# Where the output layers' seven products are added up: through copies and GpSimd, or straight from the accumulators on VectorE

## The chip, the cores and the metric

The kernel runs on one core of one Trainium2 chip. A core has five engines that work side by side, each through a queue of its own in order: TensorE (PE; matrix products, whose weight loads the profile lists as PEld), VectorE (DVE), ScalarE (ACT), GpSimd (POOL) and SyncE (SP), which here issues nearly all DMAs. Products land in PSUM, in eight banks of 128 x 512 float32; the other data live in SBUF. The metric is the device time of one execution in microseconds; lower is better.

## The reference, cut to what matters

One layer of a hybrid decoder runs over 1024 prompt columns and 8 sample columns (1032 in all, held as features x columns). Two of its four steps are SwiGLU networks with a residual:

```python
def swiglu(x, wi, wo):
    g, u = jnp.split(x @ wi, 2, axis=-1)
    return (jax.nn.silu(g) * u) @ wo

x = layer_norm(ALPHA * x + 0.5 * swiglu(x, ffn1_wi, ffn1_wo), ln_g[0], ln_b[0])
...
x = layer_norm(ALPHA * x + 0.5 * swiglu(x, ffn2_wi, ffn2_wo), ln_g[2], ln_b[2])
```

D_MODEL is 1024, the hidden width 2816. The change is in the output layer, the product with `wo`, and in how its result reaches the scaled residual `ALPHA * x`.

## The kernel before

**Precision.** Every float32 operand is split into a rounded part and a remainder ("hi" and "lo"), and each product is three matmuls: hi·hi, hi·lo, lo·hi (lines 432 to 434 in `product`, 172 to 174 in `unit`). Splitting costs a ScalarE cast (L258, L148, L588) and a VectorE subtraction (L259, L149, L589).

**Seven products in place of eight.** Most layers treat a 2 x 2 arrangement of blocks by a Strassen-Winograd scheme: two halves of the output features (i = 0, 1) and two column blocks (s and s + 2) from seven products instead of eight. There are four column blocks (`BLK4`, of 256, 260, 256 and 260 columns), so one "pair" treats s = 0 and s = 1: seven products, each for two s. `wcomb` makes the seven weight tiles of a pair from four raw blocks: seven splits, two VectorE sums (L267, L270) and two GpSimd ones (L268, L275).

**A pair before (`pair`).** Products 0, 2 and 5 accumulate in one bank A, products 4 and 6 in one bank E, products 1 and 3 have banks of their own (`aux`). Partial sums of A and E are needed too, so ScalarE copies them out to SBUF ("snapshots", L450, L457, L461, L465). The four outputs of an s are each a VectorE sum of a snapshot and a bank:

- output 0, block s: snapshot of P0, plus P1 (L454)
- output 1, block s: A = P0 + P2 + P5, less the snapshot of P3 (L469)
- output 1, block s + 2: A plus the snapshot of P4 (L470)
- output 0, block s + 2: E = P4 + P6, plus the snapshot of P0 + P2 (L474)

Banks: tag `mm` has four, `aux` three, `pn` one. `pair` takes its long accumulators A and E with `mm`, four per pair, so A of the next pair takes the bank of this pair's A. `unit_ps` hands out `mm` four times of five and `pn` the fifth time.

**The output layer (`ffn`, `segment`).** The hidden rows come back from HBM in groups of two or three pairs of 128-row tiles (`groups`), already in the seven combined forms, and are split (`split_load`, L588 and L589). Each group adds to all 1024 output features in four segments of 256 (n = 0 to 3); each segment loads its raw weights (L603), combines them and runs one pair, whose products are three or two tiles deep, so nine or six matmuls for each product and s. The residual stands in eight tiles `RT`, loaded (L595) and scaled by ALPHA on ScalarE (L596). The `out` of a segment lets VectorE write the output into a temporary tile and GpSimd add that to the residual (L610). There are three groups in each of two networks, hence 24 such pairs with eight outputs each. The rest of the hidden rows is added by plain products after that, in `ounit`, where VectorE adds the bank to the residual directly (L632).

A scheduler that simulates the engines' time line orders the instructions of each queue; `tc.high_priority()` puts what stands in it ahead of other work that is ready. Waits between engines are added from the data each touches; a whole bank counts as one.

Of the kernel before, what the change touches and what calls it, by code (L numbers as in the profile page):

```python
# [12 lines left out]
OP = mybir.AluOpType  # L13
# [17 lines left out]
BN = (256, 260)  # L31
BM = 260
BLK4 = [(i // 2 * HW + i % 2 * BN[0], BN[i % 2]) for i in range(4)]
# [3 lines left out]
def F_(ap):  # L37
    return ap.bitcast(F32)
# [25 lines left out]
def layer_kernel(ctx: ExitStack, tc: tile.TileContext, I, O):  # L64
    nc = tc.nc
    V, S, G, T, DQ = nc.vector, nc.scalar, nc.gpsimd, nc.tensor, nc.sync
# [10 lines left out]
    def gen(i, dt=F32, n=NT):  # L77

        tag = f"a{i}" if isinstance(i, int) else i
        return sb.tile([128, 1024 if tag in WN else 4 * BM], dt, name=tag, tag=tag)[:, :1024 if tag in WN else n]  # L80
# [14 lines left out]
    def tmp(n=BM):  # L95
        return tmpp.tile([128, BM], F32, name="tmp", tag="tmp")[:, :n]
# [3 lines left out]
    def mm(n=512):  # L100
        return psp.tile([128, 512], F32, name="mm", tag="mm", bufs=NMM)[:, :n]

    def unit_ps(n=512):

        turn["n"] += 1
        return mm(n) if turn["n"] % 5 else psp.tile([128, 512], F32, name="pn", tag="pn", bufs=1)[:, :n]
# [3 lines left out]
    def aux(n=512):  # L110
        return psp.tile([128, 512], F32, name="aux", tag="aux", bufs=7 - NMM)[:, :n]
# [20 lines left out]
    def slot():  # L132
        s = ring["slots"][ring["i"] % len(ring["slots"])]
        ring["i"] += 1
        return gen(s, R)
# [27 lines left out]
    def wrow(w, rows, half, dst=None):  # L163

        t = [wload(w[r:r + 128, half * 512:(half + 1) * 512].rearrange("p (k n) -> p k n", n=128), 4, 128,
                   gen(dst[i], R) if dst else None) for i, r in enumerate(rows)]
        return [[(hi[:, j, :], lo[:, j, :]) for hi, lo in t] for j in range(4)]
# [15 lines left out]
    def bs(t, b, blk=BLK):  # L183
        c0, n = blk[b]
        return t[:, c0:c0 + n]
# [17 lines left out]
    def xparts(X7, j, kp):  # L203
        t = X7[j][kp // 2]
        return t[:, 2 * (kp % 2)], t[:, 2 * (kp % 2) + 1]
# [43 lines left out]
    def wcomb(raws):  # L249

        lo_, up = raws
        g = lo_.shape[1]
        a11, a21, a12, a22 = lo_[:, :, 0:128], lo_[:, :, 128:256], up[:, :, 0:128], up[:, :, 128:256]

        def put(src):
            s = slot()
            hi, lo = (s[:, i * 512:i * 512 + g * 128].rearrange("p (k n) -> p k n", n=128) for i in range(2))
            S.copy(hi, src)  # L258
            V.tensor_tensor(lo, src, F_(hi), op=OP.subtract)  # L259
            return hi, lo  # L260

        def fresh():
            return rawp.tile([128, 512], F32, name="raw", tag="raw")[:, :g * 128].rearrange("p (k n) -> p k n", n=128)

        s1, s2, s3 = fresh(), fresh(), fresh()
        out = [put(a11)]
        V.tensor_tensor(s1, a21, a22, op=OP.add)  # L267
        G.tensor_tensor(s3, a11, a21, op=OP.subtract)  # L268
        out.append(put(a12))
        V.tensor_tensor(s2, s1, a11, op=OP.subtract)  # L270
        out.append(put(s2))
        out.append(put(a22))
        out.append(put(s1))
        s4 = fresh()
        G.tensor_tensor(s4, a12, s2, op=OP.subtract)  # L275
        out.append(put(s3))
        out.append(put(s4))
        return out
# [150 lines left out]
    def product(ps, w, xs, start, stop):  # L429
        for kp, (xh, xl) in enumerate(xs):  # L430
            wh, wl = (t[:, kp] for t in w)
            T.matmul(ps, wh, xh, start=start and kp == 0, stop=False, skip_group_check=True)  # L432
            T.matmul(ps, wh, xl, start=False, stop=False, skip_group_check=True)  # L433
            T.matmul(ps, wl, xh, start=False, stop=stop and kp == len(xs) - 1, skip_group_check=True)  # L434
# [3 lines left out]
    def pair(ws, XS, subs, out, first=False):  # L438

        live = {}  # L440

        def step(j, s):
            w = ws[j]
            xs = XS(j, s) if callable(XS) else [xparts(XS[s], j, kp) for kp in range(4)]
            P = live.setdefault(s, {})
            snap = [SN["v"][i][s] for i in range(4)]
            if j == 0:
                P["A"] = mm(BN[s])
                product(P["A"], w, xs, True, False)
                order_["snap"] = S.copy(snap[0], P["A"]).ins  # L450
            elif j == 1:
                ps = aux(BN[s])
                product(ps, w, xs, True, True)
                out(0, s, lambda d: V.tensor_tensor(d, snap[0], ps, op=OP.add))  # L454
            elif j == 2:
                product(P["A"], w, xs, False, False)
                order_["snap"] = S.copy(snap[1], P["A"]).ins  # L457
            elif j == 3:
                ps = aux(BN[s])
                product(ps, w, xs, True, True)  # L460
                order_["snap"] = S.copy(snap[2], ps).ins  # L461
            elif j == 4:
                P["E"] = mm(BN[s])
                product(P["E"], w, xs, True, False)
                order_["snap"] = S.copy(snap[3], P["E"]).ins  # L465
            elif j == 5:
                A = P["A"]
                product(A, w, xs, False, True)
                out(1, s, lambda d: V.scalar_tensor_tensor(d, snap[2], -1.0, A, op0=OP.mult, op1=OP.add))  # L469
                out(1, s + 2, lambda d: V.tensor_tensor(d, snap[3], A, op=OP.add))  # L470
            else:
                E = P["E"]
                product(E, w, xs, False, True)
                out(0, s + 2, lambda d: V.tensor_tensor(d, snap[1], E, op=OP.add))  # L474


        for j, s in [(j, s) for js in ((0, 1), (2, 3, 4, 5, 6)) for s in subs for j in js] if first else \
                [(j, s) for j in range(7) for s in subs]:
            step(j, s)
            with tc.issue_after(order_["snap"]):  # L480
                for f in beside.pop(0) if beside else ():
                    f()

    def ffn(wi, wo, l, XS, enter, xlate, raws, sgs, RTs, res, groups, plains, tail, extra=None):
# [37 lines left out]
        def wi_raw(p, k):  # L522
            i = 2 * p + k
            return wraw(wi, k * FF + p * 256, raws[2 * (i % 2):2 * (i % 2) + 2])
# [51 lines left out]
        for p in range(1, NHID // 2):  # L576
            for k in range(2):
                w = w0 if p == 1 and k == 0 else wcomb(wi_raw(p, k))
# [13 lines left out]
        RT = []  # L592
# [5 lines left out]
        def segment(ps_, parts, n, i):  # L598
            g = len(ps_)
            rw = []  # L600
            for q in range(2):
                t = gen(raws[2 * (i % 2) + q])[:, :g * 256].rearrange("p (k n) -> p k n", n=256)
                DQ.dma_start(t, wo[ps_[0] * 256:(ps_[0] + g) * 256, n * 256:(n + 1) * 256].rearrange(  # L603
                    "(k t p) n -> t p k n", t=2, p=128)[q])
                rw.append(t)

            def out(i, c, fn):
                t, r = tmp(BN[c % 2]), bs(RT[2 * n + i], c, BLK4)
                fn(t)
                G.tensor_tensor(r, r, t, op=OP.add)  # L610

            pair(wcomb(rw), lambda j, s: [tuple(bs(u, s, BLK4) for u in parts[j, k]) for k in range(g)], (0, 1), out)

        i = 0
        for ps_, slots in groups:
            parts = {}
            for j in range(7):
                for k, p in enumerate(ps_):
                    t = gen(slots[j * len(ps_) + k], R)
# [14 lines left out]
        for gi, rows_ in enumerate(plains):  # L634
# [10 lines left out]
            else:  # L645
                if extra:
                    r = ring["slots"][ring["i"] % 9:] + ring["slots"][:ring["i"] % 9]
# [102 lines left out]
    ps = aux()  # L750
# [3 lines left out]
    ps = aux()  # L754
# [170 lines left out]
    def lin_store(dst, d, n, sm):  # L925
        for i in range(2):
# [5 lines left out]
            if sm is not None:  # L932
# [6 lines left out]
    parts = {0: [(0, 26, 27), (1, 0, 1)], 2: [(7, 31, 32), (6, 10, 11)],  # L939
             1: [(0, 2, 3), (1, 8, 9)], 3: [(7, None, None), (6, 28, 29)]}  # L940
# [13 lines left out]
    for c in (0, 2, 1, 3):  # L954
        for k in range(2):
            for i in range(2):
                if len(wp) < 4:
                    wp.append(wcol(w_in, (Q0, K0)[k] + i * 128))
                ps = unit_ps(BLK4[c][1])
# [310 lines left out]
    for i in (34, 29, 20, 21):  # L1270
        t = gen(i, R, 4 * BM).rearrange("p (i t e) -> p i t e", i=2, e=BM)[:, :, :, 0:258]
# [126 lines left out]
    def wa_in(t, m):  # L1398
        s = gen((18, 28, 23)[m % 3]).rearrange("p (d n) -> p d n", n=516)
        DQ.dma_start(s[:, 0], ascr[m][:, half_cols(t)])  # L1400
        DQ.dma_start(s[:, 1], tbscr[m][:, half_cols(t)])
        return s, wcol(I["w_a"][0], m * 128)
# [34 lines left out]
    ps = aux()  # L1437
# [25 lines left out]
    for m in range(0, 8, 2):  # L1463
        u = [wa_in(1, m + i) for i in range(2)]
# [10 lines left out]
    for m in range(8):  # L1475
        for b in range(3):
            ps = unit_ps(BLK[b][1])
            unit(ps, wa[m // 4][m % 4], cols(MH[:K2], ML[:K2], b))
            r = bs(r2[m], b)
            V.scalar_tensor_tensor(r, r, ALPHA, ps, op0=OP.mult, op1=OP.add)  # L1480
    rows = [k * 128 for k in range(K2, 8)]
    w = wrow(w_mix, rows, 0, r_[0:5] + [18])
# [280 lines left out]
    t = gen(21, R)  # L1763
# [51 lines left out]
```

## Time and profile before

| | |
|---|---|
| time of three runs | 2703.46, 2705.56, 2705.60 us; median 2705.56 |
| profiled execution | 2706.57 us, of which the span of the profile is 2704.8 |
| granted TensorE clock | 0.996 of full speed |
| the 24 GpSimd-added pairs | L610 runs from 467.9 to 638.2 us and from 2324.5 to 2506.7 us, 96 times in each |

The span runs from the first to the last instruction of the profile; the rest of the execution lies around it. A row of grouped instructions gives line, engine, operation, output and inputs, shape and count, then busy time in us and the mean of one in ns, then the engine's idle time just before them with what ended it.

### The profile page before, as it was taken

The numbers are of one execution on the slowest core, as the hardware profiler recorded it, in microseconds if no ns is written. First come the engines' busy times: TensorE is split into PE (matmuls) and PEld (weight loads), VectorE is DVE, ScalarE is ACT, GpSimd is POOL, SyncE is SP. The second block draws the span as 40 slices with busy tenths as digits, with TensorE's granted clock in tenths as the row PEclk, the third lists the DMA queues.
The fourth block names the chain that finished last, engine by engine and source line by source line (L and its number), as shares of the span: only waits on it lengthen the run. The fifth ranks groups of instructions, "written<-read, shape, count | busy, mean of one in ns | idle before, by whom it ended". The sixth has DMA issues, their size and how long they took to land.

```text
span 2704.8 us, 56720 instructions
## 1 busy us (share of the span) xinstructions
PE 2647.3 (98%) x21775; PEld 2610.3 (97%) x21775; DVE 1856.5 (69%) x3932; ACT 1341.6 (50%) x3031; POOL 830.1 (31%) x840
## 2 busy tenths in 40 slices
PE   9999999999999999999999999999999999999998
PEld 9999999999999999999999999999999999999888
DVE  6755556887885756646666677758855555788887
ACT  5544446554554445446666555425544444655351
POOL 2222221565421111111111334323322222465554
PEclk9999999999999999999999999999999999999999
DMA  6333236432332434236657776731433323643211
GB/s 206 103 108 107 89 104 209 145 120 69 102 107 88 122 98 126 79 88 181 183 176 230 244 231 220 249 100 32 161 100 106 102 90 109 214 150 119 81 46 58
DMA packets 311928, 355.18 MB, mean 131 GB/s; under 512 B 28536, under 2 KB 246344, under 8 KB 311656
## 3 DMA queue, kind: packets, MB, share of 16 engines
q1 hardware_dynamic: 289336, 330.30, 38.4%
q10 hardware_dynamic: 22320, 21.26, 2.7%
q8 instruction: 170, 2.79, 0.4%
q14 instruction: 102, 0.84, 0.1%
HBM read 246.09 MB, written 105.42 MB: 130 GB/s over the span
## 4 chain that ended last, share of the span: by engine, by line
PE 37%; DVE 6%; DMA 4%; issue 2%; ACT 2%; POOL 1%; SPq 0%; DVEq 0%; ACTq 0%; POOLq 0%
PE mm L432 5%; PE mm L433 5%; PE mm L434 5%; PE mm L172 4%; PE mm L174 4%; PE mm L173 4%; PE aux L433 2%; PE aux L434 2%; PE aux L432 2%; PE pn L174 1%; PE pn L172 1%; DMA a<-in_w_in_dram 1%; PE pn L173 1%; DVE a L212 1%; DMA a<-yscr 1%
## 5 line engine op out<-in xcount | busy, mean ns | idle before, releaser
L432 PE MATMUL mm<-a,w 128*128 128x256 f32 (+1 forms) x2402 | 680.5, 284 | 9.4 <-DVE tmp L470 5.9
L433 PE MATMUL mm<-a,w 128*128 128x256 f32 (+1 forms) x2402 | 676.8, 282 | 1.2 <-DVE a L212 1.2
L434 PE MATMUL mm<-a,w 128*128 128x256 f32 (+1 forms) x2402 | 675.2, 281 | 0.0
L432 PEld LDWEIGHTS mm<-a,w 128*128 128x128 f32 x2402 | 452.6, 188 | 15.9 <-DVE tmp L470 7.6
L433 PEld LDWEIGHTS mm<-a,w 128*128 128x128 f32 x2402 | 453.0, 189 | 2.1 <-DVE a L212 1.6
L434 PEld LDWEIGHTS mm<-a,w 128*128 128x128 f32 x2402 | 452.6, 188 | 0.1
L275 POOL TENSOR_TENSOR raw<-a,raw 128x512 f32<-128x512 f32 (+2 forms) x98 | 125.4, 1279 | 949.5 <-issue 443.9
L259 DVE TENSOR_TENSOR w<-raw,w 128x512 fp32r<-128x512 f32 (+2 forms) x258 | 185.6, 721 | 203.5 <-ACT w L258 201.1
L432 PE MATMUL aux<-a,w 128*128 128x260 f32 (+1 forms) x1000 | 283.1, 283 | 3.9 <-DVE a L454 3.0
L433 PE MATMUL aux<-a,w 128*128 128x260 f32 (+1 forms) x1000 | 282.1, 282 | 0.0
L434 PE MATMUL aux<-a,w 128*128 128x260 f32 (+1 forms) x1000 | 282.1, 282 | 0.0
L432 PE MATMUL mm<-a,e 128*128 128x256 f32 (+1 forms) x812 | 230.1, 283 | 1.6 <-DVE tmp L474 1.1
L433 PE MATMUL mm<-a,e 128*128 128x256 f32 (+1 forms) x812 | 229.0, 282 | 0.8 <-DVE a L212 0.8
L434 PE MATMUL mm<-a,e 128*128 128x256 f32 (+1 forms) x812 | 228.6, 281 | 0.0
L610 POOL TENSOR_TENSOR a<-a,tmp 128x256 f32<-128x256 f32 (+1 forms) x192 | 178.9, 959 | 86.8 <-DVE tmp L454 37.8
L174 PE MATMUL mm<-a,w 128*128 128x256 f32 (+4 forms) x715 | 201.5, 285 | 0.0
L172 PE MATMUL mm<-a,w 128*128 128x256 f32 (+3 forms) x671 | 191.7, 287 | 4.0 <-ACT w L148 1.7
L432 PEld LDWEIGHTS aux<-a,w 128*128 128x128 f32 x1000 | 188.9, 189 | 5.4 <-DVE a L454 4.0
L258 ACT CAST w<-a 128x512 fp32r<-128x512 f32 (+2 forms) x200 | 117.5, 587 | 149.7 <-PE mm L434 93.6
L173 PE MATMUL mm<-a,w 128*128 128x256 f32 (+3 forms) x671 | 190.6, 285 | 0.0
L434 PEld LDWEIGHTS aux<-a,w 128*128 128x128 f32 x1000 | 189.1, 189 | 0.0
L433 PEld LDWEIGHTS aux<-a,w 128*128 128x128 f32 x1000 | 189.1, 189 | 0.0
(508 smaller groups left out, 7790.9 us busy)
## 6 DMA issues: line engine op xcount, KB each, us to landing
a<-in_ffn_wi_dram SPq DMA_DIRECT2D x80, 512.0 KB
a<-in_w_in_dram SPq DMA_DIRECT2D x68, 512.0 KB
a<-hsum SPq DMA_DIRECT2D x119, 258.0 KB
hsum<-a SPq DMA_DIRECT2D x68, 258.0 KB
a<-in_ffn_wo_dram SPq DMA_DIRECT2D x40, 384.0 KB
a<-in_state_C_dram ACTq DMA_DIRECT2D x32, 256.0 KB
out_dram<-a ACTq DMA_DIRECT2D x32, 256.0 KB
raw<-in_w_b_dram SPq DMA_DIRECT2D x32, 256.0 KB
```

The source lines that it names most:

```text
L172: T.matmul(ps, wh, xh, start=(i == 0), stop=False)
L173: T.matmul(ps, wh, xl, start=False, stop=False)
L174: last = T.matmul(ps, wl, xh, start=False, stop=(i == n - 1))
L212: order_["lo"] = V.tensor_tensor(dst[1], src, F_(dst[0]), op=OP.subtract).ins
L258: S.copy(hi, src)
L259: V.tensor_tensor(lo, src, F_(hi), op=OP.subtract)
L275: G.tensor_tensor(s4, a12, s2, op=OP.subtract)
L432: T.matmul(ps, wh, xh, start=start and kp == 0, stop=False, skip_group_check=True)
L433: T.matmul(ps, wh, xl, start=False, stop=False, skip_group_check=True)
L434: T.matmul(ps, wl, xh, start=False, stop=stop and kp == len(xs) - 1, skip_group_check=True)
L610: G.tensor_tensor(r, r, t, op=OP.add)
```

## The change

`segment` no longer uses `pair`. It runs the same 14 products in the same order and adds every accumulator, or partial accumulator, straight into the residual on VectorE, at high priority: product 0 into output 0 of block s, product 1 too; A after product 2 into output 0 of block s + 2; product 3 subtracted from output 1 of block s; product 4 into output 1 of block s + 2; A after product 5 into both blocks of output 1; E after product 6 into output 0 of block s + 2. The snapshots, temporaries and GpSimd additions of these pairs are gone. A and E come from `unit_ps`, so from five banks in turn. The pairs of other layers keep `pair`.

```diff
-            def out(i, c, fn):
-                t, r = tmp(BN[c % 2]), bs(RT[2 * n + i], c, BLK4)
-                fn(t)
-                G.tensor_tensor(r, r, t, op=OP.add)
-
-            pair(wcomb(rw), lambda j, s: [tuple(bs(u, s, BLK4) for u in parts[j, k]) for k in range(g)], (0, 1), out)
+            w = wcomb(rw)
+
+            def add(i, c, ps, op=OP.add):
+                r = bs(RT[2 * n + i], c, BLK4)
+                with tc.high_priority():
+                    V.tensor_tensor(r, r, ps, op=op)
+
+            A, E = {}, {}
+            for j, s in [(j, s) for j in range(7) for s in range(2)]:
+                if j in (0, 4):
+                    (E if j else A)[s] = unit_ps(BN[s])
+                ps = (aux(BN[s]) if j % 2 and j < 5 else E[s] if j in (4, 6) else A[s])
+                product(ps, w[j], [tuple(bs(u, s, BLK4) for u in parts[j, k]) for k in range(g)],
+                        j not in (2, 5, 6), j not in (0, 2, 4))
+                if j == 3:
+                    add(1, s, ps, OP.subtract)
+                elif j == 5:
+                    add(1, s, ps)
+                    add(1, s + 2, ps)
+                else:
+                    add(int(j == 4), s + 2 if j in (2, 4, 6) else s, ps)
```

## The prediction

> **What bounds the kernel now.** I read the page's busy time first, then the table by stretch around the two output layers, then what TensorE waited for in them.
>
> ```profile
> PE 2647.3 (98%) x21775; PEld 2610.3 (97%) x21775; DVE 1856.5 (69%) x3932; ACT 1341.6 (50%) x3031; POOL 830.1 (31%) x840
> ```
>
> TensorE (PE) is busy for 98% of the span, so the change can only pay where TensorE stands still. The changed code runs in two places: 12 pairs of column blocks from about 455 to 640 us (first output layer), 12 from about 2319 to 2507 us (second). The table by stretch (length, then busy time and instruction count of PE, PEld, VectorE, ScalarE, GpSimd) cuts the first where its pairs shrink from three tiles deep to two.
>
> ```profile
> 480.00:590.00 110.00, 106.98 (x893) 106.17 (x892) 94.20 (x158) 61.02 (x142) 69.29 (x72) 1.00 0.44 144
> 590.00:634.00 44.00, 40.25 (x320) 38.45 (x318) 38.35 (x66) 23.47 (x61) 28.13 (x34) 1.00 0.21 71
> 480.00:634.00 154.00, 147.23 (x1211) 144.63 (x1209) 132.55 (x223) 84.50 (x202) 97.43 (x105) 1.00 0.38 123
> 2345.00:2500.00 155.00, 150.21 (x1252) 149.02 (x1251) 124.08 (x207) 81.29 (x191) 93.62 (x97) 1.00 0.38 123
> ```
>
> The granted clock is 1.00 throughout, so the clock costs nothing here. VectorE (DVE) works 132.55 of 154 us in the first layer (86%) and 124.08 of 155 in the second (80%): it is the second-busiest engine, and its queue runs in order. What TensorE waited for, first layer and then second (total, times, longest):
>
> ```profile
> PE mm L432 <- DVE tmp L470: 3.6, 6, 1.2
> PE mm L432 <- DVE tmp L474: 1.8, 2, 1.1
> PE aux L432 <- DVE tmp L454: 0.9, 1, 0.9
> PE mm L432 <- ACT sreg L457: 0.5, 1, 0.5
> ...
> PE mm L432 <- DVE tmp L470: 4.5, 4, 1.3
> PE mm L432 <- ACT sreg L465: 0.3, 1, 0.3
> ```
>
> The chief row is L470, the last read of accumulator A: 10 stalls, 8.1 us, because the next pair's A wants that bank. One of them, from the timelines of PE, VectorE and GpSimd (start, duration):
>
> ```profile
> 524.52 0.28 PE L434 MATMUL aux<-a,w 128*128 128x260 f32 x1
> 525.83 0.39 PE L432 MATMUL mm<-a,w 128*128 128x260 f32 x1 [1.03 <-DVE tmp L470]
> ...
> 522.97 1.12 DVE L589 TENSOR_TENSOR a<-a 128x516 fp32r<-128x516 f32 x1
> 524.01 1.09 DVE L259 TENSOR_TENSOR w<-raw,w 128x384 fp32r<-128x384 f32 x1
> 525.02 0.41 DVE L469 SCALAR_TENSOR_TENSOR tmp<-sreg,mm 128x260 f32<-128x260 f32 x1
> 525.36 0.41 DVE L470 TENSOR_TENSOR tmp<-sreg,mm 128x260 f32<-128x260 f32 x1
> ...
> 522.80 1.89 POOL L610 TENSOR_TENSOR a<-a,tmp 128x256 f32<-128x256 f32 x2 [0.96 <-DVE tmp L469]
> ```
>
> The reads sat behind two subtractions of 1.12 and 1.09 us that ran beside two GpSimd additions. Matmul durations overlap, so stalls are better counted from starts:
>
> ```profile
> 495.41 0.28 PE L432 MATMUL aux<-a,w 128*128 128x260 f32 x1
> ...
> 496.48 0.28 PE L432 MATMUL mm<-a,w 128*128 128x256 f32 x1
> ```
>
> Nine matmuls of 260 columns take 1.07 us start to start, with 256 columns 256/260 of that: 0.118 us each on average. At that pace 893, 320 and 1252 matmuls need 105.4, 37.8 and 147.7 us; of the three stretches TensorE therefore loses **4.6, 6.2 and 7.3 us, 18.1 in all**. Idle time alone says 3.0 + 3.8 + 4.8 = 11.6 (a stall of 1.03 us shows 1.31 − 0.12 = 1.19 between starts). Between 11.6 and 18.1 lies the most that the change can remove there.
>
> **The change part by part.** A pair is seven products for each of two column blocks. *Removed per pair:* eight copies of partial sums on ScalarE, eight GpSimd additions, and the second VectorE operand from the copies. *Added:* VectorE goes from eight instructions that read an accumulator to sixteen. Products, weights and DMAs stay; nothing moves past SP's or GpSimd's queue.
>
> ScalarE and GpSimd first.
>
> ```profile
> L450 ACT COPY sreg<-mm 128x260 f32<-128x260 f32 (+1 forms) x21 | 7.8, 373 | 10.1 <-PE mm L434 9.2 <-DVE tmp L469 0.8
> ...
> L610 POOL TENSOR_TENSOR a<-a,tmp 128x260 f32<-128x260 f32 (+1 forms) x86 | 78.7, 942 | 30.6 <-DVE tmp L469 15.3 <-DVE tmp L454 9.1 <-DVE tmp L474 6.1
> ```
>
> In 154 us of the first layer ScalarE loses about 86 copies × 0.373 = 32 us and GpSimd 78.7 of its 97.43 us (81%). Neither sets the end (84.50 and 97.43 busy of 154), so by themselves both count nothing; what is late next is VectorE.
>
> VectorE pays. The same form, accumulator added into a resident tile, already runs at L632:
>
> ```profile
> L632 DVE TENSOR_TENSOR a<-a,mm x71: 401/420/542, 638.7 to 2561.7; 128x256 f32<-128x256 f32 x26, 128x260 f32<-128x260 f32 x26, 128x384 f32<-128x384 f32 x13, 128x264 f32<-128x264 f32 x6
> ```
>
> It lasts 0.42 us, but back to back such instructions start 0.34 us apart (525.02 and 525.36 above). There are as many new ones as there were GpSimd additions: 86 × 0.34 = **29.2 us more** for VectorE in the first layer's stretch, 80 × 0.34 = 27.2 in the second's.
>
> It gets part of that back, since its subtractions run longer beside GpSimd. Their rows between 480 and 634 us, and the shortest of each kind:
>
> ```profile
> L589 DVE TENSOR_TENSOR a<-a 128x516 fp32r<-128x516 f32 x36 | 30.5, 864 | 2.5 <-ACT a L588 2.1
> L259 DVE TENSOR_TENSOR w<-raw,w 128x384 fp32r<-128x384 f32 (+1 forms) x27 | 18.6, 693 | 6.5 <-ACT w L258 5.5 <-PE mm L434 1.1
> L259 DVE TENSOR_TENSOR w<-a,w 128x384 fp32r<-128x384 f32 (+1 forms) x21 | 18.0, 857 | 0.1
> L270 DVE TENSOR_TENSOR raw<-raw,a 128x384 f32<-128x384 f32 (+1 forms) x10 | 8.0, 797 | 0.0
> L267 DVE TENSOR_TENSOR raw<-a,a 128x384 f32<-128x384 f32 (+1 forms) x9 | 7.2, 799 | 3.3 <-POOL raw L275 3.2
> ...
> L589 DVE TENSOR_TENSOR a<-a x119: 677/692/1515, 430.0 to 2454.5; 128x516 fp32r<-128x516 f32 x119
> L259 DVE TENSOR_TENSOR cd<-raw,cd 128x384 fp32r<-128x384 f32 x4 | 2.2, 550 | 1.6 <-ACT cd L258 1.6
> ```
>
> Against 0.677 and 0.550 us undisturbed: 36 × 0.187 + 27 × 0.143 + 21 × 0.307 + 10 × 0.247 + 9 × 0.249 = 6.7 + 3.9 + 6.4 + 2.5 + 2.2 = 21.7 us. That is a lower bound, because some of the last 67 are only 256 wide; were all of them, an undisturbed one would last 0.55 × 256/384 = 0.37 us (an estimate) and the sum be 33.8. L610 is 81% of GpSimd's time, so **17.6 to 27.4 us come back**. I take 24, nearer the upper end since whole pairs are 256 wide in the second stretch. VectorE then needs 132.55 + 29.2 − 24 = 138 us, against 142.9 us of matmuls (1211 × 0.118): 97%. The ends are 134.4 and 144.2, and 161.8 if the lengthening has another cause. In the second layer, with the same return for each addition, it needs 124.08 + 27.2 − 22 = 129 of 147.7 (87%).
>
> [...]
>
> Waits. *Bank release:* long accumulators now rotate through five banks, four of them taken per pair, so the next pair's first A finds a bank free since the pair before last, and its second waits for a read four products back instead of three. That is the L470 stall, and it goes. *New waits:* product 2 adds into A, so it must wait for the addition after product 0, and product 6 likewise for that after product 4. ScalarE did these reads before (0.5 and 0.3 us of stalls); now they stand in VectorE's queue. That makes four waits per pair, with three products of cover: 3.2 us at depth three, 2.1 at depth two. Behind a late one TensorE holds everything. I price a stall at 0.81 us (8.1 / 10) plus the 0.26 that idle time hides (1.19 + 0.10 for the slow restart, against 1.03): 1.07 us. Unseen in this trace, their number is bounded by 0 and all 96; the additions are put at high priority and the subtractions ahead of them get shorter, so I take three, 3.2 us. *The residual tile* must be there for the first addition: it is.
>
> ```profile
> 453.58 1.07 ACT L596 ACTIVATE a<-a 128x1032 f32<-128x1032 f32 x1 [0.16 <-DMA a<-xscr]
> ...
> 464.89 0.63 ACT L450 COPY sreg<-mm 128x256 f32<-128x256 f32 x2
> ```
>
> Scaled by 454.7 us in the first layer, the first tile is ready ten microseconds before the first product's sum is read.
>
> **The sum.** Stalls removed where VectorE has room: 4.6 + 7.3 = 11.9. From 590 to 634 us, depth two, VectorE is at 38.35 of 44 and has the same work left over for less TensorE time: I count nothing of the 6.2. Less 3.2 for new stalls: −8.7. The span of 2704.8 becomes 2696.1; the profiled execution took 2706.57, 1.8 more than its span and 1.0 more than the median of 2705.56. So 2696.1 + 1.8 − 1.0 = **2696.9 us**.
>
> **The rivals.** *Slower: VectorE's additions become the tight wait.* L470 stalled 10 of its 48 times under a cover of three products. If the 80 new waits at depth three do so at that rate (17) and half the 16 at depth two (8), that is 25 × 1.07 = 26.8 us against 18.1 removed: 2705.6 + 8.7 = 2714 us. It decides above 17 stalls of 96. For it: VectorE at 97%. Against: shorter subtractions, priority.
>
> *No change: VectorE is simply full in the first layer*, its 144.2 us at the low return taking whatever TensorE saves, and only the second gains, 7.3 − 3.2: 2701.5 us. [...]
>
> *More: nothing is late any more.* All 18.1 us go: 2687.5 us. It needs the full return of shared time.
>
> **How the numbers follow.** Forecast 0.45, full VectorE 0.24, slower 0.18, all gone 0.13. A measurement of this kernel can tell about 0.2% (5.4 us) from no change: faster 0.45 + 0.13 = 0.58, same 0.24, slower 0.18. The range runs from just under the all-gone case to just short of the slow one, 2686 to 2713.
>
> **What would show it.** Right: no stall on the last reader of A; L589 near 0.70 and L259 at 384 near 0.55 us; GpSimd's time in 480 to 634 down to about 19 us; VectorE at 134 to 144 us there. Wrong: waits of mm on the new addition in more than 17 places, subtractions still at 0.85 us, or waits of TensorE on L259 or L149, the weights that VectorE would then bring late.

## The result, and the profile after

The changed kernel takes 2692.17 us (median of five executions, 2685.85 to 2695.54) against 2705.56 for the kernel before (2703.46 to 2707.96): a ratio of 0.9948, with a 95% interval of 0.9932 to 0.9964. That is 13.4 us off; 8.7 were forecast. A second set of the same kernel (e5 below) gave 2691.71 and 0.995 [0.9938, 0.9961]. The profiled execution took 2685.85 us, with a span of 2684.0: it was the fastest of the five, 6.3 below the median, so its time is not compared with the 2706.57 of before.

First the page's busy time:

```profile
PE 2638.3 (98%) x21775; PEld 2604.1 (97%) x21775; DVE 1871.4 (70%) x4124; ACT 1287.8 (48%) x2839; POOL 652.8 (24%) x648
```

TensorE has the same 21775 matmuls. VectorE gained 192 instructions (eight for each of 24 pairs) but only 15 us of busy time; ScalarE and GpSimd each lost 192 instructions. Next the table by stretch in the first output layer, with the columns as before (length; busy time and count of PE, PEld, VectorE, ScalarE, GpSimd; granted clock):

```profile
480.00:590.00 110.00, 107.79 (x898) 106.65 (x897) 97.89 (x216) 47.20 (x89) 14.12 (x14) 1.00 0.45 148
590.00:634.00 44.00, 43.54 (x356) 42.45 (x357) 41.36 (x106) 13.97 (x29) 5.46 (x8) 1.00 0.28 87
480.00:634.00 154.00, 151.33 (x1253) 149.10 (x1253) 139.25 (x321) 61.18 (x118) 19.58 (x22) 1.00 0.40 130
```

At 0.118 us per matmul, TensorE now loses 110 − 898 × 0.118 = 4.0 us in the first stretch (4.6 before) and 44 − 356 × 0.118 = 2.0 in the second (6.2 before). Nearly all of this layer's gain lies behind the point where the pairs shrink to two tiles. VectorE is at 139.25 of 154 us, 90%. Its groups there:

```profile
L612 DVE TENSOR_TENSOR a<-a,mm 128x256 f32<-128x256 f32 (+1 forms) x108 | 42.3, 412 | 7.0 <-PE mm L434 6.8
L589 DVE TENSOR_TENSOR a<-a 128x516 fp32r<-128x516 f32 x34 | 24.8, 741 | 2.2 <-ACT a L588 2.2
L612 DVE TENSOR_TENSOR a<-a,aux 128x260 f32<-128x260 f32 (+1 forms) x43 | 17.2, 412 | 1.4 <-PE aux L434 1.3
...
L259 DVE TENSOR_TENSOR w<-a,w 128x384 fp32r<-128x384 f32 (+1 forms) x21 | 10.2, 490 | 0.4 <-ACT w L258 0.2
L612 DVE TENSOR_TENSOR a<-a,pn 128x260 f32<-128x260 f32 (+1 forms) x25 | 10.1, 412 | 0.9 <-PE pn L434 0.9
```

L612 is the new addition, 176 times in this stretch. The subtractions of L589 went from a mean of 0.864 to 0.741 us, those of the weights (`w<-a,w`) from 0.857 to 0.490. Much of the idle time ahead of L612 is now spent waiting for TensorE, which is what one wants to see. What TensorE waited for, first layer:

```profile
PE mm L432 <- DVE a L612: 2.0, 4, 0.8
PE pn L432 <- DVE a L612: 0.3, 1, 0.3
PE aux L432 <- DVE a L612: 0.2, 1, 0.2
```

And from 2290 to 2500 us, the second (L172 is a matmul of the plain products behind the pairs):

```profile
PE mm L432 <- DVE a L612: 2.4, 5, 0.8
...
PE mm L172 <- DVE a L612: 0.8, 1, 0.8
...
PE pn L432 <- DVE a L612: 0.3, 1, 0.3
```

So 13 stalls wait for the new addition, 6.0 us of idle time in all, 0.46 each. (In the second list five more, 1.8 us, wait for additions of the plain products, and aren't shown.) Before, the rows shown ahead of the result have 13 stalls on VectorE's reads as well (ten on L470, two on L474, one on L454), 10.8 us, 0.83 each: the stalls became shorter, not fewer. One of them, from the timelines of TensorE and VectorE (start, duration):

```profile
529.38 0.28 PE L434 MATMUL mm<-a,w 128*128 128x260 f32 x1
530.43 0.36 PE L432 MATMUL mm<-a,w 128*128 128x256 f32 x1 [0.77 <-DVE a L612]
...
528.19 0.68 DVE L589 TENSOR_TENSOR a<-a 128x516 fp32r<-128x516 f32 x1
528.80 0.54 DVE L259 TENSOR_TENSOR w<-a,w 128x384 fp32r<-128x384 f32 x1
529.27 0.68 DVE L589 TENSOR_TENSOR a<-a 128x516 fp32r<-128x516 f32 x1
529.87 0.41 DVE L612 TENSOR_TENSOR a<-a,mm 128x260 f32<-128x260 f32 x1
```

It is the same picture as the stall shown of before, with shorter subtractions: no instruction here is stretched (0.68 and 0.54 us are the undisturbed lengths), yet three of them stand ahead of the addition.

The columns tell what kind of stall it is. A new wait, such as that of product 2 for the addition after product 0, lies within one accumulator, so the addition and the product have equally many columns, 256 for s = 0 and 260 for s = 1. A bank that is handed on goes to the other s here: four of the five banks are taken per pair, so a bank moves on by one place in the order A, A, E, E (s = 0, 1, 0, 1) from pair to pair, and the three `aux` banks alternate likewise. Above, a product of 256 columns waits for an addition of 260: it waits for a bank. In the timelines that holds for 10 of the 13 stalls, some 5.1 of the 6.0 us. Only three (at 592.95, 2366.59 and 2428.80 us; 0.9 us together) have equal columns and so are new waits. The stall on `pn`, of which there is one bank, can be followed whole:

```profile
517.84 0.28 PE L434 MATMUL pn<-a,w 128*128 128x260 f32 x1
527.01 0.35 PE L432 MATMUL pn<-a,w 128*128 128x256 f32 x1 [0.31 <-DVE a L612]
...
526.45 0.41 DVE L612 TENSOR_TENSOR a<-a,pn 128x260 f32<-128x260 f32 x1
```

The first row is the last matmul of product 5 into an A, the last row the fourth and last addition that reads this A, 8.3 us after that matmul ended. TensorE did eight other products (72 matmuls) in between and still came to a bank that wasn't free. The remaining long stalls lie at 527 to 530, 587 to 593, 2366 to 2372 and 2429 to 2434 us, where VectorE splits the next group's hidden rows (L589).

### The profile page after: what moved, and what is told of

It is laid out like the page before. It is cut to its first block, busy times and chain, and to the rows that moved or that the text cites. A ratio compares the mean times of both kernels' runs of the same rounds, so it can differ in the third digit from the quotient of the medians.

```text
span 2684.0 us, 56381 instructions
## 1 busy us (share of the span) xinstructions
PE 2638.3 (98%) x21775; PEld 2604.1 (97%) x21775; DVE 1871.4 (70%) x4124; ACT 1287.8 (48%) x2839; POOL 652.8 (24%) x648
## 4 chain that ended last, share of the span: by engine, by line
PE 79%; DVE 9%; DMA 5%; ACT 2%; issue 2%; POOL 1%; SPq 0%; ACTq 0%; DVEq 0%; POOLq 0%
PE mm L432 13%; PE mm L433 13%; PE mm L434 13%; PE aux L432 5%; PE aux L434 5%; PE aux L433 5%; PE mm L172 5%; PE mm L174 5%; PE mm L173 5%; PE pn L172 1%; PE pn L173 1%; PE pn L174 1%; DVE a L212 1%; DVE a L589 1%; DVE w L259 1%
## 5 line engine op out<-in xcount | busy, mean ns | idle before, releaser
L432 PE MATMUL mm<-a,w 128*128 128x260 f32 (+1 forms) x2313 | 654.9, 283 | 3.4 <-DVE a L612 2.5
L433 PE MATMUL mm<-a,w 128*128 128x260 f32 (+1 forms) x2313 | 651.0, 282 | 0.9 <-DVE a L212 0.9
L434 PE MATMUL mm<-a,w 128*128 128x260 f32 (+1 forms) x2313 | 649.9, 281 | 0.0
L432 PEld LDWEIGHTS mm<-a,w 128*128 128x128 f32 x2313 | 435.3, 188 | 9.0 <-issue 3.7
L433 PEld LDWEIGHTS mm<-a,w 128*128 128x128 f32 x2313 | 435.7, 188 | 1.5 <-DVE a L212 1.3
L434 PEld LDWEIGHTS mm<-a,w 128*128 128x128 f32 x2313 | 435.3, 188 | 0.1
L259 DVE TENSOR_TENSOR w<-raw,w 128x512 fp32r<-128x512 f32 (+2 forms) x258 | 174.6, 678 | 189.5 <-ACT w L258 188.2
L432 PE MATMUL mm<-a,e 128*128 128x260 f32 (+1 forms) x785 | 222.5, 283 | 0.9 <-DVE a L612 0.6
L433 PE MATMUL mm<-a,e 128*128 128x260 f32 (+1 forms) x785 | 221.2, 282 | 0.7 <-DVE a L212 0.7
L434 PE MATMUL mm<-a,e 128*128 128x260 f32 (+1 forms) x785 | 220.8, 281 | 0.0
L174 PE MATMUL mm<-a,w 128*128 128x256 f32 (+3 forms) x739 | 208.0, 284 | 0.2 <-DVE w L149 0.2
L172 PE MATMUL mm<-a,w 128*128 128x260 f32 (+4 forms) x695 | 198.0, 286 | 3.2 <-DVE a L647 1.7
L173 PE MATMUL mm<-a,w 128*128 128x260 f32 (+4 forms) x695 | 197.0, 285 | 0.0
L258 ACT CAST w<-raw 128x512 fp32r<-128x512 f32 (+2 forms) x258 | 152.2, 591 | 65.6 <-PE aux L434 21.6
```

The lines of the kernel that those rows point to most:

```text
L172: T.matmul(ps, wh, xh, start=(i == 0), stop=False)
L173: T.matmul(ps, wh, xl, start=False, stop=False)
L174: last = T.matmul(ps, wl, xh, start=False, stop=(i == n - 1))
```

## The experiments

All kernels were run with several executions beside the kernel before. Since executions of one kernel spread over some 10 us, the table also gives, from one profile of each, how long TensorE took over the same part of its work: the two output layers and the stretch of some 460 us in between in which the mixing layers run. The lengths are worked out: the time between two fixed matmul numbers (4000 to 5600, 10000 to 13800, 19400 to 21050), counted in 10 us slices of the table by stretch and interpolated. A matmul that crosses a slice's edge counts in both, alike in all kernels. In parentheses stands the part of a length that a lower granted clock accounts for: 1 minus the granted clock, times the slice, summed.

| kernel | 1st output layer | mixing | 2nd output layer | median, ratio to before [95%] |
|---|---|---|---|---|
| before | 197.1 | 464.1 (3.4) | 200.0 | 2705.56 |
| the change | 190.9 | 454.0 | 197.9 | 2692.17, 0.9948 [0.9932, 0.9964] |
| e5, the change again | 190.6 | 462.7 (3.4) | 197.6 | 2691.71, 0.995 [0.9938, 0.9961] |
| e1, GpSimd traffic back | 199.0 | 459.7 (1.7) | 203.6 | 2710.7, 1.0021 [1.0013, 1.003] |
| e2, four banks | 196.5 (1.7) | 461.9 (1.7) | 202.3 | 2700.44, 0.9988 [0.9978, 0.9999] |
| e3, banks only | 200.9 (3.4) | 468.8 (3.4) | 204.9 (5.1) | 2714.21, 1.0032 [1.002, 1.0043] |
| e4, no additions | 187.8 | 463.4 (3.4) | 194.5 (0.6) | 2686.22, 0.9931 [0.9919, 0.9943] |
| e6, first layer only | 190.8 | 454.0 | 201.0 (1.7) | 2693.74, 0.9962 [0.9947, 0.9976] |
| e7, second layer only | 196.7 | 466.8 (1.7) | 197.5 | 2704.37, 0.9996 [0.9986, 1.0005] |
| e8, bank counter only | 197.0 | 462.9 (1.7) | 199.9 | 2705.19, 1.0002 [0.9993, 1.0011] |
| e9, no priority | 190.8 | 462.6 (3.4) | 198.6 | 2693.59, 0.9964 [0.9951, 0.9978] |
| e10, counter put back | 189.9 | 455.6 | 197.9 | 2693.95, 0.9965 [0.9951, 0.9979] |
| e11, products apart | 192.2 (1.7) | 456.8 (1.7) | 199.0 | 2693.85, 0.9967 [0.9955, 0.9979] |
| e12, seven additions | 191.3 | 457.5 (1.7) | 195.8 | 2686.57, 0.9943 [0.9931, 0.9955] |

The medians of the kernel before beside them were 2703.72 (e1 to e4), 2705.3 (e5 to e8) and 2703.72 us (e9 to e12). The clock-free sum of the two output layers is the number to watch: 397.1 before, 388.8 with the change and 388.2 in its second profile, so **8.3 to 8.9 us** of the 13.4 are gained in the layers that were changed.

### What pays: VectorE's shorter work, or the banks (e1 to e4)

Theory A: the gain comes from GpSimd falling silent, since VectorE then has room and its reads come in time; the banks don't matter. Theory B: it comes from the fifth bank, which gives the reads more cover; GpSimd's traffic doesn't matter.

**e1** keeps the change and has GpSimd add again, four times for each s of a pair, so eight times per pair as before, into a temporary that nobody reads:

```diff
                     V.tensor_tensor(r, r, ps, op=op)
+                if j in (1, 5, 6):
+                    G.tensor_tensor(tmp(BN[c % 2]), r, r, op=OP.add)
```

> The changed kernel with eight idle GpSimd additions per pair put back: when an output has got one of its additions on VectorE, GpSimd adds that residual tile to itself into a temporary tile that nobody reads. Theory A (GpSimd's additions lengthened VectorE's subtractions, and that made TensorE stall): L589 at 128x516 returns from 0.74 to about 0.85 us, VectorE is overfull between 480 and 634 us, TensorE loses at least as much there as before the change, and the time is 2705 to 2715 us. Theory B (five banks in turn are what counts): the subtractions may lengthen, but the stalls stay away, 2690 to 2697 us.

2710.7 us, 18.5 above the change and slower than before. The table by stretch, VectorE's weight subtraction, and TensorE's waits in the first layer:

```profile
480.00:634.00 154.00, 146.80 (x1194) 143.01 (x1193) 146.81 (x305) 58.88 (x114) 84.29 (x106) 1.00 0.37 121
```

```profile
L259 DVE TENSOR_TENSOR w<-a,w 128x384 fp32r<-128x384 f32 (+1 forms) x21 | 15.8, 752 | 0.0
```

```profile
PE mm L432 <- DVE a L612: 5.2, 8, 1.2
```

GpSimd is back at 84.29 us and VectorE at 146.81 of 154 (95%), though it ran 16 instructions fewer here than in the change: the weights' subtraction is at 0.752 us again instead of 0.490. The subtractions of L589 only went from 0.741 to 0.770 us, not to the 0.85 that Theory A named, so not all of the time went back: 7.6 us more with 16 instructions fewer, an estimate of 13 to 16 us at 0.34 to 0.5 us for one (the distance between starts, and about the mean of all, 146.81 / 305). The output layers take 402.6 us, 13.8 more than with the change. So the return of VectorE's time is real, and without it the change loses.

**e2** keeps the change and takes A and E from the four `mm` banks:

```diff
                 if j in (0, 4):
-                    (E if j else A)[s] = unit_ps(BN[s])
+                    (E if j else A)[s] = mm(BN[s])
```

> The changed kernel with its long accumulators in four banks instead of five. Theory A: the shorter subtractions are enough, 2690 to 2697 us, as with five. Theory B: the next pair's A waits for the last read of this pair's A again, some ten stalls of a microsecond in each direction of the two layers come back, 2702 to 2707 us.

2700.44 us. The waits, first layer and then second:

```profile
PE mm L432 <- DVE a L612: 6.7, 8, 1.6
...
PE mm L432 <- DVE a L612: 7.2, 8, 1.2
```

VectorE's subtractions are short here, but 16 stalls of 0.87 us wait for L612, and the output layers take 397.1 us free of clock, as before the change. (The whole is 3.3 us faster than before, just clear of the noise; by this profile they lie outside these layers.) A, with its banks that don't matter, falls.

**e3** gives the kernel before the five banks alone:

```diff
-    def pair(ws, XS, subs, out, first=False):
+    def pair(ws, XS, subs, out, first=False, bank=None):
...
-                P["A"] = mm(BN[s])
+                P["A"] = (bank or mm)(BN[s])
...
-                P["E"] = mm(BN[s])
+                P["E"] = (bank or mm)(BN[s])
...
-            pair(wcomb(rw), lambda j, s: [...], (0, 1), out)
+            pair(wcomb(rw), lambda j, s: [...], (0, 1), out, bank=unit_ps)
```

> The kernel before, with copies, temporaries and GpSimd additions as they were, and only the long accumulators of the output layers' pairs in five banks. Theory A: VectorE is as late as before and something else waits for it, 2701 to 2706 us. Theory B: the ten stalls on L470 go, 2690 to 2698 us.

2714.21 us, slower than before, so B falls too. The waits, second layer:

```profile
PE aux L432 <- DVE tmp L454: 4.1, 2, 2.0
PE mm L432 <- DVE tmp L470: 1.4, 2, 0.7
```

The stalls on L470 shrank (4.5 us before in this layer), as B has it, but its place was taken by fewer and longer ones on L454, the read of the `aux` banks. And a pause of two microseconds can bring a cost of its own, here in the first layer (a matmul of TensorE's timeline, then the slice of 10 us that holds it):

```profile
533.13 0.39 PE L432 MATMUL aux<-a,e 128*128 128x260 f32 x1 [2.07 <-DVE tmp L454]
```

```profile
530.00:540.00 10.00, 7.93 (x54) 7.72 (x54) 10.00 (x19) 5.30 (x14) 4.16 (x4) 0.83 0.14 42
```

The granted clock of the slice is 0.83 (the last section shows what that is, matmul by matmul). Over the whole profile but its last 60 us the lower clock costs 13.6 us, against 6.8 before. In the output layers it costs 8.5 us, against nothing before; free of it they take 397.3 us, no more and no less than before.

**e4** leaves the residual additions of the 24 pairs out of the kernel before, with its four banks and its copies (so the output lacks them):

```diff
             def out(i, c, fn):
-                t, r = tmp(BN[c % 2]), bs(RT[2 * n + i], c, BLK4)
-                fn(t)
-                G.tensor_tensor(r, r, t, op=OP.add)
+                fn(tmp(BN[c % 2]))
```

> The kernel before without its GpSimd additions in the output layers (four banks, copies kept): the 24 pairs leave their outputs in the temporary tiles and the residual doesn't get them. Theory A: subtractions at 0.68 and 0.55 us, VectorE some 24 us freer in the first layer, no stalls on L470, 2685 to 2695 us, at least as fast as the changed kernel. Theory B: the stalls on L470 stay, 2701 to 2706 us.

2686.22 us. The stretch, and all that TensorE waited for in the first layer:

```profile
480.00:634.00 154.00, 153.43 (x1279) 151.94 (x1278) 110.26 (x234) 86.29 (x204) 22.01 (x23) 1.00 0.41 134
```

```profile
PE mm L432 <- ACT sreg L457: 0.3, 1, 0.3
```

With VectorE at 72%, the same four banks and three products of cover produce no stall on VectorE in the first layer; 1279 matmuls need 150.9 of the 154 us. The output layers take 381.7 us. The change reaches a bit more than half of the way from 397.1 to there.

Together: direct additions without the fifth bank are worth 0.0 us in these layers, the fifth bank without direct additions −0.2, both together 8.3 to 8.9. Neither theory stands alone. A stall needs a late read and too little cover, and at this load of VectorE (from 480 to 634 us 86% before, 88% in e2, 84% in e3) each half of the change leaves the other cause in place. That this is why the halves give nothing alone is argued from the waits; the times are measured.

### Where the gain lies (e5 to e8)

e5 is the changed kernel once more. e6 applies the change to the first output layer only (`if l == 0:`, else the old `pair` with its `out`), e7 to the second only (`if l == 2:`). e8 is the kernel before with the bank counter alone moved on, as the change moves it, so that the plain products behind these pairs meet other banks:

```diff
+            turn["n"] += 4
             pair(wcomb(rw), lambda j, s: [...], (0, 1), out)
```

> The changed kernel itself once more, with the kernel before beside it. In its first profile the two output layers were 8.3 us shorter than before (6.2 and 2.1) and the mixing layers between the 10000th and the 13800th TensorE instruction, which the change doesn't touch, 10.1 us shorter, 3.4 of them by a higher granted clock. Theory A (what the change does itself is the 8 us; the rest is chance of the run): output layers 388 to 391 us together, mixing stretch 458 to 462 us, ratio 0.995 to 0.998. Theory B (the scheduler orders the mixing layers otherwise after this change, and that is worth some 6 us every time): mixing stretch 453 to 456 us again, ratio 0.993 to 0.995.

> The change in the first output layer alone. Theory A: the first layer's stretch (4000th to 5600th TensorE instruction) takes 191 us as in the changed kernel, against 197, the second's 200 as before; the time is 5 to 7 us below before. Theory B: the mixing stretch shortens too, 10 to 13 us below before in all.

> The change in the second output layer alone. Theory A: first stretch 197 us, second (19400th to 21050th instruction) 198 us against 200, mixing stretch as before at 461 to 464; the time is 1 to 4 us below before. Theory B, in which what goes before the mixing layers matters for them, expects the same here, since nothing before them is changed; a time more than 6 us below before would speak against both.

> The kernel before, with the counter that hands out the fifth bank moved on by four in each output-layer pair, as the changed kernel moves it, and nothing else: later plain products get other banks. Theory A: nothing to gain or lose, within 3 us of before. Theory B: the mixing stretch moves by several us, down to 454, or up as in the run with five banks only (465 without its lost clock).

e6 has 0.9962, e7 0.9996, e8 1.0002: nearly all of the gain goes with the first output layer; in the second the layer itself gets 2.5 us shorter (197.5 against 200.0) and the whole shows no difference that can be told; the counter alone does nothing. e6's 10 us (0.0038 × 2705.3) are more than the 6.3 that its first output layer gains. The profiles put the rest into the mixing layers, which the change does not touch: 454.0 to 462.7 us raw in the kernels with a changed first layer (the change, e5, e6, e9 to e12) against 462.9 to 468.8 in those without (before, e3, e4, e7, e8); e1 and e2, which alter the change in both layers, have 459.7 and 461.9. But e5 has 462.7 with the same program that has 454.0 in the first profile, so part of it is the single execution. One place shows how. The chain of what ended last, around 1290 us, for the kernel before and then e5:

```profile
1294.60 5.09 DMA sm<-st
1299.79 0.42 DVE a L454
```

```profile
1285.40 5.03 DMA sm<-st
```

This DMA, of 4 KB, took 5.09 and 5.03 us (4.63 in the first profile of the change), and a VectorE instruction waits for it with all of VectorE's queue behind it. TensorE's wait at that place, for the kernel before, the first profile of the change, and e5:

```profile
PE pn L1188 <- DVE tmp L1192: 3.1, 1, 3.1
```

```profile
PE pn L1203 <- DVE tmp L1207: 1.8, 1, 1.8
```

```profile
PE pn L1203 <- DVE tmp L1207: 2.6, 1, 2.6
```

And the slice of 10 us that holds it, in the same order:

```profile
1300.00:1310.00 10.00, 7.71 (x48) 7.11 (x49) 7.41 (x17) 6.66 (x16) 2.54 (x2) 0.83 0.41 103
```

```profile
1290.00:1300.00 10.00, 10.00 (x81) 9.29 (x82) 7.79 (x17) 7.15 (x19) 2.67 (x2) 1.00 0.55 171
```

```profile
1290.00:1300.00 10.00, 7.35 (x47) 6.48 (x45) 6.07 (x15) 5.80 (x15) 2.11 (x2) 0.83 0.44 106
```

Where the pause is 2.6 or 3.1 us, the clock drops behind it and the slice holds 47 or 48 matmuls; where it is 1.8, it does not, and the slice holds 81 (the pause itself lies just ahead of it, from 1287.9 to 1290). This one place is worth about 1.7 us of clock besides the pause, and it went either way in two executions of one program. What decides it is not shown: the last section has two pauses of 1.72 us, one with half rate behind it and one without. Why kernels with the changed first layer come out shorter here more often stays open.

### Is it the order behind the layers, and which waits are left (e9 to e12)

**e9** takes the additions out of high priority; **e10** keeps the change and moves the counter on by 2 behind it, so that it stands for the later layers as it does before the change:

```diff
-                with tc.high_priority():
-                    V.tensor_tensor(r, r, ps, op=op)
+                V.tensor_tensor(r, r, ps, op=op)
```

```diff
                 i += 1
+        turn["n"] += 2
```

> The changed kernel with the additions at ordinary priority. Theory A (priority is not what pays, since these additions stand ahead of the later weights in the program anyway): 2690 to 2695 us, output layers 388 to 391 us together. Theory P (priority keeps TensorE's new waits short): more and longer waits on the addition, output layers 392 us or more, 2696 to 2702 us.

> The changed kernel, with the fifth-bank counter moved on by two after each output layer, so that plain products later get their banks in the rhythm of the kernel before (and the mixing layers' instructions most likely its order). Theory A: output layers 388 to 391 us, mixing stretch like the others, time within 2 us of the changed kernel's 2692. Theory B (the other order of the mixing layers is worth some 5 us): mixing stretch 460 us or more without lost clock, time 2695 to 2699 us.

e9: 0.9964 [0.9951, 0.9978], output layers 389.4 us: the priority is worth nothing that can be measured. e10: 0.9965 [0.9951, 0.9979], with the mixing layers at 455.6 us although the counter stands there as before: the counter is not what shortens them.

Two theories on the stalls that are left. V: VectorE is late as a whole, and a stall falls on whichever wait comes next. W: it is the tight waits that the change added, product 2 for the addition after product 0 and product 6 for that after product 4. **e11** moves them apart by another order of the products (and has the weights' sum for product 4 split earlier):

```diff
-            for j, s in [(j, s) for j in range(7) for s in range(2)]:
+            for j, s in [(j, s) for j in (0, 1, 4, 2, 3, 5, 6) for s in range(2)]:
```

> The changed kernel with the products of a pair in the order 0, 1, 4, 2, 3, 5, 6, so that between product 0 and product 2 of a block, and between 4 and 6, stand five and seven others instead of three; only 2 to 5 has three then. Theory W (the stalls that remain, about 5.5 us of idle time on the addition, are these two tight waits): most of them go, output layers 383 to 386 us together, 2686 to 2690 us. Theory V (VectorE is too full where it splits the next group, whatever the order): the waits move to product 5 or to the next pair, output layers 387 to 390 us, no change against the changed kernel.

2693.85 us, output layers 389.5. The longest wait, first layer:

```profile
PE pn L433 <- DVE a L613: 2.1, 1, 2.1
```

(L613 is this kernel's L612.) Stalls moved to other products, fewer and longer (seven on the additions, five of them with equal columns); the layers take as long as with the change. That speaks for V, and so does the trace of the change itself, in which only three of 13 stalls are waits of W's kind, and one read of VectorE comes 8 us after its product.

**e12** lowers the number of VectorE's additions from 16 to 14 per pair: product 3 uses negated weights and goes into A last, so that one addition takes P0 + P2 + P5 − P3 and none subtracts P3 alone; product 4 starts E in an `aux` bank.

```diff
+            if minus:
+                S.activation(hi, src, AF.Copy, scale=-1.0)
+                V.scalar_tensor_tensor(lo, src, -1.0, F_(hi), op0=OP.mult, op1=OP.subtract)
+                return hi, lo
...
-            for j, s in [(j, s) for j in range(7) for s in range(2)]:
+            for j, s in [(j, s) for j in (0, 1, 2, 4, 5, 6, 3) for s in range(2)]:
...
+                add(int(j in (3, 4, 5)), s + 2 if j in (2, 4, 5, 6) else s, ps)
```

> The changed kernel with one addition less: product 3 has negated weights and accumulates into A after A was added to block s + 2, so that output 1 of block s gets one addition instead of two; products in the order 0, 1, 2, 4, 5, 6, 3; E in the three aux banks. VectorE loses 24 additions of 0.34 us, 8 us, in each layer, but each pair has eight tight waits in place of four. Theory V: less VectorE work wins, output layers 382 to 386 us, 2684 to 2690 us. Theory W: more tight waits lose, output layers 390 us or more, 2693 to 2700 us.

2686.57 us, 0.9943 [0.9931, 0.9955]. The stretch and the chief wait, first layer:

```profile
480.00:634.00 154.00, 149.95 (x1245) 147.87 (x1245) 133.96 (x297) 62.31 (x118) 18.20 (x20) 1.00 0.42 134
```

```profile
PE aux L439 <- DVE a L619: 1.2, 3, 0.6
```

VectorE is down to 133.96 us. The output layers take 387.1, between what V (382 to 386) and W (390 or more) expected, and the stalls now stand above all at products in `aux` banks. In the second layer the two longest of these, 2.9 us together, wait for ScalarE's cast of the hidden rows, not for VectorE. Its interval overlaps that of the change, so it is not shown to be the better version.

## Why the prediction was right, and where it was not

The time lies inside the range and on the forecast's side, 4.7 us below the number. By its steps:

- **VectorE's return of time: right.** 24 us were taken, from 17.6 to 27.4. In 480 to 634 us there are 176 accumulator reads in place of 86; 90 × 0.34 = 30.6 us more, and 132.55 + 30.6 − 139.25 = 23.9 came back. e1, which takes the return away, is slower than before. The estimate of 0.37 us for an undisturbed subtraction of 256 columns, which set the upper end, was too low: in the change, from 455 to 640 us, the group of that form alone shows 0.412, and 0.549 at 384:

```profile
L259 DVE TENSOR_TENSOR w<-raw,w 128x384 fp32r<-128x384 f32 x20 | 10.9, 549 | 2.2 <-ACT w L258 2.2
L259 DVE TENSOR_TENSOR w<-raw,w 128x256 fp32r<-128x256 f32 x10 | 4.1, 412 | 0.0
```

- **VectorE at 134 to 144 us, GpSimd at about 19, L589 near 0.70, L259 near 0.55: right** (139.25, 19.58, 0.741, 0.549).
- **"I count nothing of the 6.2", the stretch of depth two: the term that failed most.** It lost 6.2 us and now loses 2.0. I argued that VectorE would have the same work left over for less TensorE time. But it was not full there, only late: from 600 to 640 us, where the pairs end and the plain products begin, the kernel before and the change read

```profile
600.00:640.00 40.00, 37.52 (x299) 36.03 (x300) 34.35 (x62) 19.26 (x48) 29.67 (x35) 1.00 0.28 88
```

```profile
600.00:640.00 40.00, 40.00 (x337) 39.49 (x336) 34.35 (x87) 12.84 (x24) 5.82 (x8) 1.00 0.38 113
```

  with 34.35 us of VectorE in both, and in the second no idle time of TensorE at all. The same busy share, from more and shorter instructions, no longer stalls TensorE.
- **"4.6 + 7.3" removed: too much.** The stretch of depth three in the first layer gained 0.6 of its 4.6, and the second layer 2.1 to 2.5 in all. From 2345 to 2400 us the kernel before, then the change:

```profile
2345.00:2400.00 55.00, 52.45 (x434) 51.67 (x433) 44.52 (x77) 30.05 (x70) 30.99 (x32) 1.00 0.45 145
```

```profile
2345.00:2400.00 55.00, 53.49 (x442) 52.70 (x442) 48.48 (x106) 23.20 (x45) 6.55 (x6) 1.00 0.47 152
```

  Eight matmuls more in 55 us, 0.9 us; the stretch still loses 55 − 442 × 0.118 = 2.8.
- **Bank release, "That is the L470 stall, and it goes": wrong.** Ten of the 13 stalls still wait for a bank, with some 5.1 us of idle time against 8.1 on L470. With the 0.26 that idle time hides, that is an estimate of 10 × 0.77 = 7.7 us where the prediction has nothing, and it is why the 4.6 and 7.3 didn't go. The cover grew as the prediction says, but where VectorE splits the next group's rows its reads come later than that: the stall on `pn` has eight products under it. It also waits for the last reader of an A, so "no stall on the last reader of A" didn't come true.
- **"Three new stalls" at 1.07 us: the count held, the size was too high.** By their columns three stalls are waits within one accumulator, 0.3 us of idle time each; with the hidden 0.26, an estimate of 1.7 us against the 3.2 counted.
- **The sum.** In the changed layers the forecast was 8.7 us and the profiles have 8.3 to 8.9: the terms erred in both directions and cancelled, so that this sum came out is luck. The 4.7 us by which the median is lower than forecast lie outside these layers, mostly with the first layer's change (e6), and were in no term.
- **The rivals.** "VectorE's additions become the tight wait" fell: three such stalls, where 17 would have decided. In e2, with one bank fewer, 16 stalls bring the layers back to 397.1 us, close to that number; but there a bank goes on to the same s, so the columns don't tell which kind they are. "VectorE simply full" fell in the place where it was expected, and all-gone fell with the 13 stalls.

## What to carry to other kernels

When a busy in-order engine, here VectorE at 84 to 90%, releases another's buffers, look at how late its reads come and how much work covers them together: here shortening the queue (e2) or adding a bank (e3) alone gave nothing in these layers, and both gave 8.3 to 8.9 us. Taking an addition from a third engine can leave the busy one hardly busier, if it was slowed by the third's work, here by some 0.28 us for each addition; price both sides from the undisturbed rows of the same trace. One row of waits can hold two kinds, for a bank and within an accumulator; tell them apart, here by the columns, before saying what is left. A stretch whose busy share looks full may be late only at some points, so count the stalls there before writing its gain off.

## What the runs showed of the hardware

- **Some pauses of TensorE were followed by 3.41 us at half rate, others were not.** TensorE's timeline of the kernel before, around the pause shown above:

```profile
1302.29 0.39 PE L1188 MATMUL pn<-a,a 128*16 128x256 f32 x2 [3.12 <-DVE tmp L1192]
1302.52 0.28 PE L432 MATMUL aux<-a,w 128*128 128x260 f32 x1
1302.64 0.28 PE L433 MATMUL aux<-a,w 128*128 128x260 f32 x1
...
1303.42 0.42 PE L432 MATMUL aux<-a,w 128*128 128x260 f32 x1
1303.63 0.42 PE L433 MATMUL aux<-a,w 128*128 128x260 f32 x1
...
1306.56 0.28 PE L432 MATMUL mm<-a,w 128*128 128x256 f32 x1
1306.67 0.29 PE L433 MATMUL mm<-a,w 128*128 128x256 f32 x1
```

  The first matmuls behind the pause still start 0.12 us apart; from about 1303.0 to 1306.4 they start 0.22 apart, and then 0.12 again. That is 3.4 us at half rate (the granted clock from 1303.03 to 1306.44 us is 0.50): 1.7 us lost, and in a slice of 10 us the 0.83 that the table shows. All pauses over 1.5 us in the traces of the kernel before and of the change, without the last 60 us of each, and one each of e5 and e3:

  | trace | pause and when it ended | half rate |
  |---|---|---|
  | before | 2.08 us, 1238.1 | from 1238.2 |
  | before | 3.12 us, 1302.3 | from 1303.0 |
  | before | 1.68 us, 1729.2 | no |
  | before | 2.93 us, 2586.7 | from 2586.4 |
  | before | 1.72 us, 2637.0 | from 2637.6 |
  | the change | 1.80 us, 1290.0 | no |
  | the change | 1.73 us, 1909.5 | no |
  | the change | 2.98 us, 2567.2 | from 2568.1 |
  | the change | 1.72 us, 2617.6 | no |
  | e5 | 2.65 us, 1293.1 | from about 1294.3 |
  | e3 | 2.07 us, 533.1 | from about 533.8 |

  In the kernel before and the change each of these stretches lasted 3.41 us at a granted clock of 0.50. Those of the kernel before began 64.86, 1283.41 and 51.20 us after each other, which is 19, 376 and 15 times 3.413. In the 3.41 us ahead of them TensorE was idle for 2.08, 2.67, 2.68 and 1.72 us, ahead of that of the change for 2.44. So a pause cost up to 1.7 us more or nothing more: half rate followed all six of 2 us or more in the table and one of the five of 1.68 to 1.80 us. What decides among these, and whether a longer pause can go without, is not shown.
- **GpSimd's additions cost VectorE some 0.28 us each here, by an estimate** (23.9 us returned for 86 additions of 0.942 us). The subtractions of L589 went from a mean of 0.864 to 0.741 us, the weights' from 0.857 to 0.490; in the stall shown ahead of the result, two subtractions beside 1.89 us of GpSimd took 1.12 and 1.09 us, 0.44 and 0.54 more than undisturbed. The figure isn't a constant: in e1, by the estimate above, 84 such additions took 0.15 to 0.19 us each.
- **A VectorE subtraction of L259 lasted 0.412 us at 256 columns and 0.549 at 384** (rows of the change above): 1.07 ns per column and 0.138 us fixed, by the two rows. Scaling by columns alone, as the prediction did, is 0.04 us short.
